# Second attention of a two-block model: probabilities transposed by VectorE in 32x32 squares and carried between partitions by DMAs, in place of TensorE transposes

## The chip, the cores and the metric

The kernel runs on one core of a Trainium2 chip. TensorE (PE, with its weight loads PEld), VectorE (DVE), ScalarE (ACT), GpSimd (POOL) and SyncE (SP, here only a queue that issues DMAs) each work through a list of instructions in order, and wait for one another by semaphores. The metric is the device time of one execution in microseconds (us), taken as the median of several runs.

## The reference

Two blocks of a model on one sequence of 512 tokens with 1024 channels, all in float32. The first block (gated mixing, a long convolution, a stick-breaking attention, a feed-forward layer) is not touched. The second, cut to what matters:

```python
h = rms_norm_2(x, norm_g); proj = h @ w_in            # u, g_rnn, q, k, v, g_attn, m_rnn, m_attn
u = causal_depthwise_conv_2(u, conv_w, conv_b)        # 4 taps
y_rnn = rg_lru(u, ...) * silu(g_rnn)                  # two 128x128 products per block, then a scan
q, k = rope(q), rope(k)                               # 16 query heads, 4 key/value heads
# per block of 128 queries: the 128 keys of the block and the 128 before it, a window of 128
p = exp(scores - m); probs = p / (sum(p) + exp(sink - m))
y_attn = einsum("bnkgqj,bnjkd->bnqkgd", probs, v) * silu(g_attn)
merged = sigmoid(m_rnn) * (y_rnn @ w_rnn_out) + sigmoid(m_attn) * (y_attn @ w_attn_out)
x = rms_norm_2(x + merged @ w_o)
```

## The kernel before

Activations lie as tiles of 128 channels by 512 tokens. Every dense product runs as three float32r matmuls (`mm3`, L293 to L295): the high part of the weight with the high and the low part of the activation, and the low part of the weight with the high part. `project` makes one 128x512 output tile out of eight (or four) weight tiles, so 24 matmuls.

**Weights.** They come as 216 chunks of eight 128x128 tiles (512 KB), in the order of use. `w_load` (L153) issues the DMA of one chunk on the SP queue into one of two `raw` buffers; `w_split` has ACT write the high part `wh` (L169) and DVE the low part `wl` (L170), with three buffers of each. `take` asks for the splits of three chunks and the loads of five. One chunk feeds 24 matmuls.

**Background work.** Attention is written as Python generators (`window_attention`), eight units: two pairs of key/value heads (`kvp`) by four blocks of queries (`n`). A unit makes the scores of two heads (`e`) in two PSUM tiles each (L955, L956), copies them to `S4` (the names `p`), takes maxima, exponentials (L972) and the quotient (L978), transposes the 128x128 probabilities on TensorE (L986, `ident` as the other operand, four per head), copies them out of PSUM (`own`, L987, on ACT; `prev`, L990, on DVE, with a mask, where n > 0), and multiplies with the values (L1000); L1004 puts the result into `ya`. `tick`, called in every `project` after each four weight tiles, advances the generators by a budget (`clk["rate"]`), against the cost that each `yield` names; its second number is a delay in ticks. `finish(*units)` stands ahead of the use of `ya`.

**The order on each engine** is set by a scheduler that works through the instructions by a priority in the order of the program; `urgent()` raises the priority of what stands in it. The stage after the attention starts, L1060 on, has nine rounds: `project` for `u`, a convolution of four taps (L1064 on ACT, three L1066 on DVE), `split` into `uh`, `ul` (L286 and L289), `project` for the gate (`silu2`, L1012, L1013), and `lru` of the round before, whose two products take `uh`, `ul`. Two loops of eight rounds follow, `br` 0 on `yr`, `br` 1 on `ya`, and the last product.

Of the kernel before, what the change touches and what calls it, by code (L numbers as in the profile page):

```python
# [8 lines left out]
F32 = mybir.dt.float32  # L9
F32R = mybir.dt.float32r  # L10
BF16 = mybir.dt.bfloat16
AF = mybir.ActivationFunctionType
ALU = mybir.AluOpType

P = 128
T = 512
# [110 lines left out]
def tile_hybrid_two_block(ctx, tc, xT, wts, prm_d, row_d, sgw_d, rope_d, sink_d, out):  # L127
    nc = tc.nc
    V, A, G, PE = nc.vector, nc.scalar, nc.gpsimd, nc.tensor
# [10 lines left out]
    def bank(tag="mm"):  # L140
        return pm.tile([P, 512], F32, tag=tag, name=nm(tag))
# [101 lines left out]
    ident = const.tile([P, P], F32, name="ident")  # L243
# [10 lines left out]
    class Area:  # L254
# [10 lines left out]
        def tmp(self, dt=F32):  # L265
            return self.tile([P, T], dt)
# [4 lines left out]
    area = [None]  # L271
# [4 lines left out]
    def urgent():  # L276

        return tc.high_priority(offset=URGENT)

    def pr(name, i=0):  # L280
        c = PO[name] + i
        return prm0[:, c : c + 1] if c < n0 else prm[:, c : c + 1]

    def split(src, h, l, eng="a"):
        if eng == "a":
            A.copy(out=h, in_=src)  # L286
        else:
            V.tensor_copy(out=h, in_=src)
        V.tensor_tensor(out=l, in0=src, in1=h.bitcast(F32), op=ALU.subtract)  # L289
# [91 lines left out]
    ps = bank("aux")  # L381
# [114 lines left out]
    for i in range(4):  # L496
        ps = project(hh)
        sg = tmp()
        A.activation(sg, ps, AF.Sigmoid)
        ps = project(hh)  # L500
# [5 lines left out]
    for m in range(4):  # L506
        ps = project(hh)
# [37 lines left out]
    for base in (0, 32):  # L545
# [5 lines left out]
            out=blk, in_=blk, compare_op=ALU.is_ge, fill=0.0, base=0, pattern=[[P, 4], [1, P]],  # L551
# [3 lines left out]
            out=blk, in_=blk, compare_op=ALU.is_ge, fill=0.0, base=63, pattern=[[-P, 4], [-1, P]],  # L555
# [181 lines left out]
    for br, y in enumerate((ya4, acc)):  # L737
# [3 lines left out]
        for m in range(KT):  # L741
            sg = gate(m, br, tmp())
            ps = project(ys)
# [13 lines left out]
    for m in range(KT):  # L757
        ps = project(ys)
# [18 lines left out]
    for m in range(KT):  # L777
        x = tmp()
        nc.sync.dma_start(out=x, in_=xT[m])
        ps = project(mgs)  # L780
# [35 lines left out]
    for m in range(NFF):  # L816
        if m == EARLY:
            finish(norm_task)
        a = up_conv(m, m < EARLY)
        A.activation(a, a, AF.Silu)  # L820
        b = up_conv(m + NFF, m < EARLY)
# [11 lines left out]
    for m in range(KT):  # L833
        ps = project(ffs)
# [6 lines left out]
    VV = area[0].tile([P, NT, 256], F32, "v")  # L841
# [23 lines left out]
    with urgent():  # L865
        ps, pt = mean_sq(S, tok=True, tag="mm")
# [73 lines left out]
    def window_attention(kvp, n):  # L940
        nk = P if n == 0 else 2 * P
        qs = slice(n * P, (n + 1) * P)
        ks = slice((n + 1) * P - nk, (n + 1) * P)
        prs = []
        for e in range(2):
            kv = 2 * kvp + e
            S4 = area[0].tile([P, 4, P], F32, "p")
            prs.append(S4)
            m4, nm4, es, sm = (area[0].tile([P, 4], F32, "s") for _ in range(4))
            per = T // nk  # L950
            for j0 in range(0, 4, per):
                ps = bank("aux")
                for d in range(per):
                    z, q = ps[:, d * nk : (d + 1) * nk], QS[kv][:, j0 + d, qs]
                    PE.matmul(z, lhsT=q, rhs=KS[kvp][:, 2 * e, ks], start=True, stop=False)  # L955
                    PE.matmul(z, lhsT=q, rhs=KS[kvp][:, 2 * e + 1, ks], start=False, stop=True)  # L956
                z = ps.rearrange("p (d k) -> p d k", d=per)
                x = S4[:, j0 : j0 + per]
                if n == 0:
                    V.tensor_tensor(out=x, in0=z, in1=mask[:, 0:1].to_broadcast([P, 4, P]), op=ALU.add)  # L960
                else:
                    A.copy(out=x, in_=z[:, :, P:nk])
                    V.copy_predicated(x, mask[:, 1:2].bitcast(mybir.dt.int32).to_broadcast([P, 2, P]), z[:, :, 0:P])
                yield 0.5, 0
            V.tensor_reduce(out=m4, in_=S4, axis=mybir.AxisListType.X, op=ALU.max)
            sk = sink[:, kv * 4 : kv * 4 + 4]
            V.scalar_tensor_tensor(out=m4, in0=m4, scalar=0.125, in1=sk, op0=ALU.mult, op1=ALU.max)
            V.tensor_scalar(out=nm4, in0=m4, scalar1=-1.0, scalar2=None, op0=ALU.mult)  # L968
            V.tensor_tensor(out=es, in0=sk, in1=m4, op=ALU.subtract)
            A.activation(es, es, AF.Exp)  # L970
            for j in range(4):
                A.activation(  # L972
                    S4[:, j], S4[:, j], AF.Exp, scale=0.125, bias=nm4[:, j : j + 1], accum_out=sm[:, j : j + 1]
                )
            yield 0.95, 1
            V.tensor_tensor(out=sm, in0=sm, in1=es, op=ALU.add)
            V.reciprocal(out=sm, in_=sm)
            V.tensor_tensor(out=S4, in0=S4, in1=sm.unsqueeze(2).to_broadcast([P, 4, P]), op=ALU.mult)  # L978
            yield 0.9, e


        own, prev = [tmp(), tmp()], []
        for e in range(2):
            ps = bank("aux")
            for j in range(4):
                PE.transpose(ps[:, j * P : (j + 1) * P], prs[e][:, j], ident)  # L986
            A.copy(out=own[e], in_=ps)  # L987
            if n > 0:
                prev.append(tmp())
                V.tensor_tensor(  # L990
                    out=prev[e].rearrange("p (a b) -> p a b", a=4), in0=ps.rearrange("p (a b) -> p a b", a=4),
                    in1=mask[:, 2:3].to_broadcast([P, 4, P]), op=ALU.mult,
                )
        yield 1.4 if n else 0.1, 2
        po = bank("aux")
        sums = [(VV[:, n], own)] + ([(VD[:, n - 1], prev)] if n else [])
        for i, (v, w) in enumerate(sums):
            for e in range(2):
                f = kvp * P + e * 64
                PE.matmul(  # L1000
                    po[e * 64 : e * 64 + 64], lhsT=v[:, f : f + 64], rhs=w[e], start=i == 0, stop=i == len(sums) - 1
                )
        y = ya[kvp][:, :, qs]
        V.scalar_tensor_tensor(  # L1004
            out=y, in0=po.rearrange("p (a b) -> p a b", a=4), scalar=0.5, in1=y, op0=ALU.mult, op1=ALU.mult
        )
        yield 0.66, 5
# [52 lines left out]
    for m in range(9):  # L1060
        if m < 8:
            ps = project(h3)
            u = area[0].tile([P, T], F32, "u")
            A.activation(u, ps, AF.Identity, scale=pr("conv_w_2", 24 + m), bias=pr("conv_b_2", m))  # L1064
            for d in (1, 2, 3):
                V.scalar_tensor_tensor(  # L1066
                    out=u[:, d:T], in0=ps[:, 0 : T - d], scalar=pr("conv_w_2", (3 - d) * 8 + m), in1=u[:, d:T],
                    op0=ALU.mult, op1=ALU.add,
                )
            uh, ul = area[0].tile([P, T], F32R, "u"), area[0].tile([P, T], F32R, "u")  # L1070
            split(u, uh, ul)
            silu2(project(h3), yr[m // 4][:, m % 4])
        if late:
            pair.append(lru(*late))
            if len(pair) == 2:
                recurrence(pair)
                pair = []
        late = (m, u, uh, ul)
# [122 lines left out]
```

## Time and profile before

| | us |
|---|---|
| median of 3 runs (1288.71 to 1289.31) | 1288.73 |
| the profiled execution's own time | 1289.3 |
| its span in the profile | 1287.5 |
| PE busy | 1273.9 |
| DVE busy | 869.8 |
| ACT busy | 599.5 |

The span is what the profiler saw from the first instruction to the last; 1.8 us of the execution's own time lie around it. Engines are busy beside one another, so the busy times do not add up. Matmuls are pipelined: each is shown as lasting some 0.39 us, while one starts every 0.23 us, so the cost of a matmul is read from start to start.

### The profile page before, as it was taken

Reading aid. Unit: us, or ns where it says so; the run is one execution under the profiler, and the core shown is the slowest. Engines: PE = TensorE matmul, PEld = TensorE weight load, DVE = VectorE, ACT = ScalarE, POOL = GpSimd, SP = SyncE. Lnnn points to the kernel's source line nnn. Section 1 sums busy time; section 2 is a strip of 40 time slices with the busy share of each in tenths; the row PEclk is TensorE's granted clock in tenths of the full one; section 3 lists DMA queues with packets and bytes.
Section 4 is the critical chain, followed back from the end, with each engine's and each line's share of the span. In section 5 each row is a group of like instructions: output and inputs, shape, how many; then the busy total and the mean of one; then the engine's idle time right before and its main releaser. Section 6 shows DMA issues by size and latency. Waiting matters only on the chain.

```text
span 1287.5 us, 15405 instructions
## 1 busy us (share of the span) xinstructions
PE 1273.9 (99%) x5890; PEld 1034.6 (80%) x5890; DVE 869.8 (68%) x1313; ACT 599.5 (47%) x964; POOL 46.7 (4%) x85
## 2 busy tenths in 40 slices
PE   9999999999999999999999999999999999999997
PEld 7888787778888888888888888888878777788886
DVE  6899998776447597666664333897678895633355
ACT  6733555546324464444443222644568874532232
POOL 0100004320000000000000000000000000000000
PEclk9999999999999999999999999999999999999999
DMA  6332322212333323223333333323223222223341
GB/s 212 131 98 85 96 82 82 66 50 82 98 107 123 131 82 112 91 95 97 97 98 106 115 115 116 99 90 115 83 82 97 67 82 66 81 84 98 131 131 66
DMA packets 39114, 126.80 MB, mean 98 GB/s; under 512 B 4480, under 2 KB 6656, under 8 KB 39040
## 3 DMA queue, kind: packets, MB, share of 16 engines
q1 hardware_dynamic: 37808, 124.76, 30.5%
q8 instruction: 46, 0.75, 0.2%
q10 hardware_dynamic: 1232, 1.05, 0.2%
q14 instruction: 28, 0.23, 0.1%
HBM read 121.60 MB, written 4.19 MB: 98 GB/s over the span
## 4 chain that ended last, share of the span: by engine, by line
PE 96%; DVE 2%; ACT 1%; issue 0%; DMA 0%; POOL 0%; DVEq 0%; SPq 0%; ACTq 0%
PE mm L293 29%; PE mm L294 29%; PE mm L295 29%; PE aux L1000 1%; PE aux L638 1%; PE aux L293 1%; PE aux L295 1%; PE aux L294 1%; PE aux L669 1%; PE aux L955 1%; PE aux L956 1%; PE aux L682 1%; PE aux L986 1%; DVE t L1136 0%; DVE wl L170 0%
## 5 line engine op out<-in xcount | busy, mean ns | idle before, releaser
L293 PE MATMUL mm<-g,wh 128*128 128x512 f32 x1592 | 624.1, 392 | 0.2 <-ACT g L286 0.2
L294 PE MATMUL mm<-g,wh 128*128 128x512 f32 x1592 | 620.6, 390 | 0.0
L295 PE MATMUL mm<-g,wl 128*128 128x512 f32 x1592 | 620.4, 390 | 0.0
L170 DVE TENSOR_TENSOR wl<-raw,wh 128x1024 fp32r<-128x1024 f32 (+1 forms) x212 | 257.8, 1217 | 217.6 <-ACT wh L169 216.9
L169 ACT CAST wh<-raw 128x1024 fp32r<-128x1024 f32 (+1 forms) x211 | 221.4, 1049 | 373.3 <-PE mm L294 276.0
L293 PEld LDWEIGHTS mm<-g,wh 128*128 128x128 f32 x1592 | 299.0, 188 | 67.1 <-issue 4.6
L295 PEld LDWEIGHTS mm<-g,wl 128*128 128x128 f32 x1592 | 299.0, 188 | 63.1 <-issue 0.3
L294 PEld LDWEIGHTS mm<-g,wh 128*128 128x128 f32 x1592 | 299.1, 188 | 60.9 <-DVE g L289 0.4
L490 DVE SCALAR_TENSOR_TENSOR g<-g,prm,g 128x505 f32<-128x505 f32 (+28 forms) x120 | 82.0, 726 | 0.8
L286 ACT CAST g<-t 128x512 fp32r<-128x512 f32 x46 | 28.2, 620 | 64.6 <-DVE t L822 54.3
L809 DVE SCALAR_TENSOR_TENSOR t<-mm,prm,t 128x511 f32<-128x511 f32 x72 | 53.7, 746 | 1.3
L289 DVE TENSOR_TENSOR g<-t,g 128x512 fp32r<-128x512 f32 x46 | 31.7, 696 | 14.3 <-ACT g L286 14.1
L286 ACT CAST g<-g 128x512 fp32r<-128x512 f32 x44 | 25.9, 621 | 24.1 <-DVE g L760 14.2
L972 ACT ACTIVATE p<-p,s 128x128 f32<-128x128 f32 x64 | 24.9, 390 | 21.7 <-DVE s L968 21.7
L820 ACT ACTIVATE t<-t 128x512 f32<-128x512 f32 x22 | 13.9, 633 | 40.4 <-DVE t L809 40.3
L656 DVE TENSOR_TENSOR_SCAN t<-t,zero 128x512 f32<-128x512 f32 (+3 forms) x32 | 27.1, 850 | 7.3 <-POOL t L651 7.2
L289 DVE TENSOR_TENSOR g<-g,g 128x512 fp32r<-128x512 f32 x44 | 28.9, 683 | 2.6 <-ACT g L286 2.1
L807 ACT ACTIVATE t<-mm,prm 128x512 f32<-128x512 f32 x36 | 27.8, 773 | 0.0
L376 ACT ACTIVATE t<-g 128x512 f32<-128x512 f32 (+1 forms) x29 | 17.2, 592 | 20.8 <-DVE g L1115 17.2
L356 ACT ACTIVATE g<-g,prm 128x512 fp32r<-128x512 f32 x24 | 17.2, 718 | 18.0 <-DVE g L768 16.9
L1097 DVE SCALAR_TENSOR_TENSOR t<-t,mm 128x512 f32<-128x512 f32 x8 | 5.5, 688 | 27.1 <-PE mm L295 27.1
L293 PE MATMUL aux<-wh,g 128*128 128x512 f32 (+1 forms) x64 | 21.8, 341 | 0.0
(266 smaller groups left out, 1201.5 us busy)
## 6 DMA issues: line engine op xcount, KB each, us to landing
raw<-in_wts SPq DMA_DIRECT2D x215, 512.0 KB, 3.6
g<-in_xT SPq DMA_DIRECT2D x8, 256.0 KB, 5.8
t<-in_xT SPq DMA_DIRECT2D x8, 256.0 KB, 3.8
spill<-g SPq DMA_DIRECT2D x8, 256.0 KB, 3.3
g<-spill SPq DMA_DIRECT2D x8, 256.0 KB, 4.4
out<-t ACTq DMA_DIRECT2D x4, 256.0 KB, 2.3
out<-t SPq DMA_DIRECT2D x4, 256.0 KB, 2.4
g<-in_row SPq DMA_DIRECT2D x1, 768.0 KB, 6.5
```

The lines of the kernel that those rows point to most:

```text
L169: A.copy(out=h[:, o : o + step], in_=raw[c][:, o : o + step])
L170: V.tensor_tensor(out=l[:, o : o + step], in0=raw[c][:, o : o + step], in1=h[:, o : o + step].bitcast(F32), op=ALU.subtract,)
L286: A.copy(out=h, in_=src)
L289: V.tensor_tensor(out=l, in0=src, in1=h.bitcast(F32), op=ALU.subtract)
L293: PE.matmul(ps, lhsT=lh, rhs=rh, start=start, stop=False)
L294: PE.matmul(ps, lhsT=lh, rhs=rl, start=False, stop=False)
L295: PE.matmul(ps, lhsT=ll, rhs=rh, start=False, stop=stop)
L490: V.scalar_tensor_tensor(out=a[:, d:T], in0=c[:, 0 : T - d], scalar=pr("cv_w", (30 - d) * 4 + i), in1=a[:, d:T], op0=ALU.mult, op1=ALU.add,)
L656: V.tensor_tensor_scan(out=R[:, 0:cx][:, ::-1], data0=F[:, 0:cx][:, ::-1], data1=zero.to_broadcast([P, cx]), initial=1.0, op0=ALU.mult, op ...
L807: A.activation(a, y, AF.Identity, scale=pr("ffn_conv_w", 88 + m), bias=pr("ffn_conv_b", m))
L809: V.scalar_tensor_tensor(out=a[:, d:T], in0=y[:, 0 : T - d], scalar=pr("ffn_conv_w", (2 - d) * 44 + m), in1=a[:, d:T], op0=ALU.mult, op1=A ...
L972: A.activation(S4[:, j], S4[:, j], AF.Exp, scale=0.125, bias=nm4[:, j : j + 1], accum_out=sm[:, j : j + 1])
```

## The change

It transposes each 128x512 tile of probabilities on DVE, in squares of 32x32, into a tile `turned`, and issues 16 DMAs from the SP queue that put the squares into their places in a tile `w`, which is `own`. `prev` is made from `w` instead of from PSUM. In units with n = 0, which have no `prev`, a copy of four columns of `w` onto themselves is left on DVE. The sum takes `prev` first. The costs and delays of the yields are new. The chain that makes `u`, `uh` and `ul` stands in `urgent()`.

```diff
-        prs = []
+        own = []
         for e in range(2):
             kv = 2 * kvp + e
             S4 = area[0].tile([P, 4, P], F32, "p")
-            prs.append(S4)
...
             V.tensor_tensor(out=S4, in0=S4, in1=sm.unsqueeze(2).to_broadcast([P, 4, P]), op=ALU.mult)
-            yield 0.9, e
-
-
-        own, prev = [tmp(), tmp()], []
+            yield 0.7, 0
+
+            turned, w = tmp(), tmp()
+            V.transpose(out=turned, in_=S4.rearrange("p a b -> p (a b)"))
+            own.append(w)
+            src, dst = (x.rearrange("p (a b) -> p a b", a=4) for x in (turned, w))
+            for i in range(4):
+                for j in range(4):
+                    nc.sync.dma_start(
+                        out=dst[32 * j : 32 * j + 32, :, 32 * i : 32 * i + 32],
+                        in_=src[32 * i : 32 * i + 32, :, 32 * j : 32 * j + 32],
+                    )
+            yield 0.7, 5 * e
+
+
+        prev = []
         for e in range(2):
-            ps = bank("aux")
-            for j in range(4):
-                PE.transpose(ps[:, j * P : (j + 1) * P], prs[e][:, j], ident)
-            A.copy(out=own[e], in_=ps)
+            w = own[e].rearrange("p (a b) -> p a b", a=4)
             if n > 0:
                 prev.append(tmp())
                 V.tensor_tensor(
-                    out=prev[e].rearrange("p (a b) -> p a b", a=4), in0=ps.rearrange("p (a b) -> p a b", a=4),
+                    out=prev[e].rearrange("p (a b) -> p a b", a=4), in0=w,
                     in1=mask[:, 2:3].to_broadcast([P, 4, P]), op=ALU.mult,
                 )
-        yield 1.4 if n else 0.1, 2
+            else:
+                w = w[:, 0, 0:P:32]
+                V.tensor_copy(out=w, in_=w)
+        yield 1.4 if n else 0.1, 1
         po = bank("aux")
-        sums = [(VV[:, n], own)] + ([(VD[:, n - 1], prev)] if n else [])
+        sums = ([(VD[:, n - 1], prev)] if n else []) + [(VV[:, n], own)]
...
-            u = area[0].tile([P, T], F32, "u")
...
+            with urgent():
+                u = area[0].tile([P, T], F32, "u")
+                A.activation(u, ps, AF.Identity, scale=pr("conv_w_2", 24 + m), bias=pr("conv_b_2", m))
...
+                uh, ul = area[0].tile([P, T], F32R, "u"), area[0].tile([P, T], F32R, "u")
+                split(u, uh, ul)
             silu2(project(h3), yr[m // 4][:, m % 4])
```

**The chain of the last `u` on DVE (m = 7).** Before, its three steps (L1066) stand apart, a split of weights (L170) and the gate's product (L1013, which waits for the `project` after the one of `u`) between them:

```order
L978 TENSOR_TENSOR p_7997<-p_7997,s_8001 128x512
L1066 SCALAR_TENSOR_TENSOR u_8099<-mm_8059,prm,u_8099 128x511
L170 TENSOR_TENSOR wl_8110<-raw_7983,wh_8109 128x1024
L1066 SCALAR_TENSOR_TENSOR u_8099<-mm_8059,prm,u_8099 128x510
L1013 SCALAR_TENSOR_TENSOR g_7255<-t_8142,mm_8108 128x512
L1066 SCALAR_TENSOR_TENSOR u_8099<-mm_8059,prm,u_8099 128x509
L1038 TENSOR_SCALAR t_8153<-t_8153,s_6344 128x512
L1045 SCALAR_TENSOR_TENSOR t_8154<-t_8154,u_7969 128x512
L289 TENSOR_TENSOR u_8105<-u_8099,u_8104 128x512
```

In the changed kernel the lines are L1078 for the three steps and L998 for `prev`:

```order
L998 TENSOR_TENSOR t_8194<-t_7791,mask_6303 128x512
L1078 SCALAR_TENSOR_TENSOR u_8154<-mm_8104,prm,u_8154 128x511
L1078 SCALAR_TENSOR_TENSOR u_8154<-mm_8104,prm,u_8154 128x510
L1078 SCALAR_TENSOR_TENSOR u_8154<-mm_8104,prm,u_8154 128x509
L1064 TENSOR_TENSOR t_8086<-t_8086,t_8085 128x512
L962 COPY_PREDICATED p_8123<-mask_6303,aux_8147 128x256
L1065 SCALAR_TENSOR_TENSOR t_8090<-t_8090,t_8086 128x512
L170 TENSOR_TENSOR wl_8165<-raw_8028,wh_8164 128x1024
L289 TENSOR_TENSOR u_8160<-u_8154,u_8159 128x512
```

The three steps stand together now, and the gate's product stands behind the whole chain.

**The SP queue at the start of the loop `br` 0.** Before, it holds nothing there but loads of chunks, one for each 24 matmuls. In the changed kernel, where t_8342, t_8425, ... are the tiles `w` of five successive heads (16 DMAs each):

```order
L986 DMA t_8342<-t_8341 32x4x32 x16
L153 DMA raw_8407<-in_wts 128x1024
L986 DMA t_8425<-t_8424 32x4x32 x16
L153 DMA raw_8485<-in_wts 128x1024
L986 DMA t_8503<-t_8502 32x4x32 x16
L986 DMA t_8561<-t_8560 32x4x32 x16
L153 DMA raw_8586<-in_wts 128x1024
L153 DMA raw_8622<-in_wts 128x1024
L986 DMA t_8778<-t_8777 32x4x32 x3
L153 DMA raw_8661<-in_wts 128x1024
```

Chunks raw_8586 and raw_8622 stand behind 48 small DMAs that follow raw_8407.

**The same place on ACT and PE.** ACT before, from the copy-out of one tile's scores (L962) to the next chunk's high part:

```order
L169 CAST wh_8651<-raw_8538 128x1024
L1092 ACTIVATE t_8599<-mm_8600 128x512
L962 COPY p_8675<-aux_8680 128x256
L962 COPY p_8675<-aux_8687 128x256
L972 ACTIVATE p_8675,s_8679<-p_8675,s_8677 128x128
L970 ACTIVATE s_8678<-s_8678 128x4
L972 ACTIVATE p_8675,s_8679<-p_8675,s_8677 128x128 x3
```

ACT in the changed kernel (L961 is the copy-out, L971 the exponentials), ahead of the chunk raw_8586:

```order
L961 COPY p_8796<-aux_8808 128x256
L961 COPY p_8878<-aux_8883 128x256
L961 COPY p_8878<-aux_8890 128x256
L971 ACTIVATE p_8725,s_8729<-p_8725,s_8727 128x128
L969 ACTIVATE s_8728<-s_8728 128x4
L971 ACTIVATE p_8725,s_8729<-p_8725,s_8727 128x128 x3
L969 ACTIVATE s_8799<-s_8799 128x4
L971 ACTIVATE p_8796,s_8800<-p_8796,s_8798 128x128 x3
L169 CAST wh_8657<-raw_8586 128x1024
```

PE in the changed kernel, the end of 32 score matmuls in a row (L954, L955; before, they come in groups of eight with dense matmuls between), one product with the values (L1011), and the next dense tile:

```order
L955 MATMUL aux_8952<-g_6391,g_6501 128x256
L1011 MATMUL aux_8689<-t_8561,v_6184 64x512
L293 MATMUL mm_8755<-g_6380,wh_8657 128x512
L294 MATMUL mm_8755<-g_6382,wh_8657 128x512
L293 MATMUL mm_8859<-g_8251,wh_8695 128x512
L295 MATMUL mm_8755<-g_6380,wl_8658 128x512
```

The scores of four heads stand together ahead of mm_8755, and its weights stand on ACT behind the exponentials of the first two of them.

## Rows read from the trace of the kernel before

**Rows 1.** The page: busy time, share, instructions; then the chain by engine.

```profile
PE 1273.9 (99%) x5890; PEld 1034.6 (80%) x5890; DVE 869.8 (68%) x1313; ACT 599.5 (47%) x964; POOL 46.7 (4%) x85
...
PE 96%; DVE 2%; ACT 1%; issue 0%; DMA 0%; POOL 0%; DVEq 0%; SPq 0%; ACTq 0%
```

**Rows 2.** Timeline of PE at four transposes: start, length (us), line, tile, count.

```profile
1117.82 0.39 PE L295 MATMUL mm<-g,wl 128*128 128x512 f32 x1
1118.05 0.60 PE L986 MATMUL aux<-ident,p 128*128 128x128 f32 x4
1118.40 0.48 PE L293 MATMUL mm<-g,wh 128*128 128x512 f32 x1
1118.72 0.40 PE L294 MATMUL mm<-g,wh 128*128 128x512 f32 x1
```

**Rows 3.** Timeline of PE at the last `u`; in brackets the idle time before.

```profile
1028.33 0.60 PE L986 MATMUL aux<-ident,p 128*128 128x128 f32 x4
1032.11 1.22 PE L293 MATMUL mm<-u,wh 128*128 128x512 f32 x2 [3.18 <-ACT u L286]
...
1035.83 0.39 PE L293 MATMUL mm<-g,wh 128*128 128x512 f32 x1
```

**Rows 4.** SP: issues back to back, one line's issues (ns), its waits.

```profile
1203.30 1.38 SPq L1104 DMA_DIRECT2D g<-spill  x3
...
L153 SPq DMA_DIRECT2D raw<-in_wts x215: 327/328/496, 2.7 to 1244.0; - x108
...
SPq L153 <- DVE wl L170: 1034.3, 200, 15.5
```

**Rows 5.** The chain that ended last, a piece of eight transposes: start, us.

```profile
926.87 0.87 PE aux L986 x8
```

**Rows 6.** Groups by line and shape, 800 to 1135 us: busy us, mean ns, idle before.

```profile
L978 DVE TENSOR_TENSOR p<-p,s 128x512 f32<-128x512 f32 x16 | 11.0, 689 | 0.4
...
L919 DVE STREAM_SHUFFLE t<-mm 128x512 f32<-128x512 f32 x10 | 7.4, 736 | 0.0
...
L169 ACT CAST wh<-raw 128x1024 fp32r<-128x1024 f32 x37 | 38.7, 1046 | 36.5 <-PE mm L294 25.0 <-issue 11.1 <-DMA raw<-in_wts 0.3
L972 ACT ACTIVATE p<-p,s 128x128 f32<-128x128 f32 x64 | 24.9, 390 | 21.7 <-DVE s L968 21.7
```

**Rows 7.** The chain that ended last, 1028 to 1035 us.

```profile
1028.31 1.13 DVE wl L170
1029.44 0.66 DVE u L1066
1030.10 0.59 DVE g L1013
1030.69 0.67 DVE u L1066
...
1034.61 0.43 PE mm L294
```

**Rows 8.** By stretch: PE, PEld, DVE, ACT, POOL busy; then PE's granted clock.

```profile
1030.00:1060.00 30.00, 27.70 (x120) 21.26 (x121) 28.30 (x50) 21.80 (x42) 0.00 (x0) 0.94 0.30 87
```

**Rows 9.** The page: DMA issues, count, KB each, median us to landing.

```profile
raw<-in_wts SPq DMA_DIRECT2D x215, 512.0 KB, 3.6
...
out<-t SPq DMA_DIRECT2D x4, 256.0 KB, 2.4
```

**Rows 10.** Timelines of PE, ACT, DVE: one tile from scores to the quotient.

```profile
1107.82 0.39 PE L955 MATMUL aux<-g,g 128*128 128x256 f32 x1
...
1108.88 0.40 PE L293 MATMUL mm<-g,wh 128*128 128x512 f32 x1
...
1111.53 0.40 ACT L972 ACTIVATE p<-p,s 128x128 f32<-128x128 f32 x1 [2.08 <-DVE s L968]
...
1113.92 0.68 DVE L978 TENSOR_TENSOR p<-p,s 128x512 f32<-128x512 f32 x1
```

**Rows 11.** The page: the queue with the shortest packets; packets, MB, share.

```profile
q10 hardware_dynamic: 1232, 1.05, 0.2%
```

More of the change, by code (lines that the diff above doesn't have):

```diff
@@ L1062, in tile_hybrid_two_block @@
             ps = project(h3)
-            u = area[0].tile([P, T], F32, "u")
[L1064 to L1071, printed above, removed]
+            with urgent():
+                u = area[0].tile([P, T], F32, "u")
+                A.activation(u, ps, AF.Identity, scale=pr("conv_w_2", 24 + m), bias=pr("conv_b_2", m))
+                for d in (1, 2, 3):
+                    V.scalar_tensor_tensor(
+                        out=u[:, d:T], in0=ps[:, 0 : T - d], scalar=pr("conv_w_2", (3 - d) * 8 + m), in1=u[:, d:T],
+                        op0=ALU.mult, op1=ALU.add,
+                    )
+                uh, ul = area[0].tile([P, T], F32R, "u"), area[0].tile([P, T], F32R, "u")
+                split(u, uh, ul)
             silu2(project(h3), yr[m // 4][:, m % 4])
```

## The prediction

> **What bounds the kernel now.** I read the page's busy times and the chain that ended last first: PE is busy for 99% of the span and makes 96% of the chain [rows 1]. So whatever leaves PE shortens the kernel, and whatever makes PE wait lengthens it; work on other engines counts only where PE waits for it. Next I read PE's timeline from 890 to 1130 us, where the eight units run. A dense matmul starts every 0.23 us there. Two things break that pace: groups of four transposes [rows 2], and one stall of 3.18 us at 1028 us, for the last `u` [rows 3]. Last I read SP, since the change puts its DMAs there: SP mostly sits waiting for DVE's split of a chunk (1034 us in 200 waits), and an issue takes 0.33 us [rows 4].
>
> **The change part by part.**
>
> *Transposes leave PE.* A group of four takes 0.35 us to the next dense matmul, which then holds PE for 0.32 instead of 0.23 us: 0.44 [rows 2]; the chain has 0.87 for two groups [rows 5]. There are 16 groups (8 units, 2 heads). The one at 1028.33 lies in the stall and is counted there. Fifteen by 0.44 are 6.6, and at some of them PE waits a little for the quotient, which goes too: I take **6.9 gained**. This is on the path in full. The VectorE page of the Trainium skill ("VectorE: DVE Perf Modes", The three transpose paths and Rules for kernel authors) speaks against the move: it gives 390 ns for a 128x128 transpose on TensorE, and advises TensorE where PSUM will do. With its 390 ns the 64 would be worth 25 us, an estimate; the rows show 0.11 us each, and the sum goes by them.
>
> *ACT loses 16 copies, DVE gains 16 transposes.* Neither bounds the stage as a whole. The nearest DVE rows are a 128x512 product (0.69) and a 128x512 shuffle (0.74) [rows 6], which start some 0.08 less than that apart; I take 0.65. It counts only inside a chain that PE waits for (below), else nothing.
>
> *The `u` chain.* Before, the three steps of the last `u` have a weight split (1.13) and the gate's product (0.59) between them, and PE waits at their end [rows 7]. The stall costs more than its 3.18: behind it matmuls start 0.43 apart [rows 7] instead of 0.23, the level of 1.2 GHz, and the granted clock of that stretch is 0.94 [rows 8]; before the fall PE had idled. Nine matmuls stand between 1032.11 and 1035.83 [rows 3]; at 0.23 behind the transposes (1028.33 + 0.44) they would end at 1030.8, so 5.0 us are lost. In the new order the steps stand together, and PE has a full `project` (24 matmuls, 5.5 us) between its matmuls for `u` and those that use it, against some 4 us of chain. I take **5.0 gained**; the low bound is 3, if DVE, on its way to the last split of `yr`, gives part back.
>
> *The 256 DMAs.* Nothing in the trace has this shape. SP issues others back to back at 1.38 us for three, so 0.475 from start to start; apart, one takes 0.33 [rows 4]. Those are the bounds for a free queue; I take 0.475, as 16 stand in a row. 16 KB should land no later than 256 KB does, in 2.4 [rows 9]. Eight can be in flight (each waits for the eighth before it), which at 2.4 us would allow 0.30 each, so issue decides. A head takes 7.6 us of SP, and is landed 10 us after its transpose. Behind these DMAs stand loads of weights, and on DVE the products for `prev` wait for the landing, with weight splits behind them. A chunk feeds PE for 5.5 us; a load can go about 13 us late before PE misses it (PE is 22 us from a chunk when its load can first go, less 3.6 to land [rows 9], 2.3 to split, and some 3 of waiting for the buffer). Units 0 to 2 stay within that: at most 32 small DMAs (15 us) stand ahead of a load, and it could go 4 us after the first. In `br` 0 five units follow one another within 100 us: 160 DMAs, 76 us of SP, in bursts. Three places come out late:
>
> 1. *Ahead of mm_8755.* Counted from the first of the 32 score matmuls: PE does eight in 1.06 us [rows 10], so is through them at 4.2, and the product with the values at 4.5. Exponentials start 3.7 after a tile's scores [rows 10], 4.1 with other tiles' rows on DVE; seven of 0.39 [rows 6] end at 6.9; the chunk's high part (1.0) is there at 7.9, its low part at 9.6, behind a quotient (0.6), the 32x32 transpose (0.65) and its own 1.13. The chunk itself lands at about 5, so here the order decides, not the landing. PE loses 5.0, and by rows 3 and 7 another 1.8 at the low clock (nine matmuls by 0.2): **6.8 lost** (5.0 if the clock holds).
> 2. *The product of unit 6.* In the same count raw_8760 can go at 16, when the chunk before the last is split; then 56 small DMAs and two loads end at 43.4 and have landed at 45.8; DVE's product ends at 46.4. PE, from 9.2 with 1.8 at the low clock, has 144 dense matmuls (32.8) and 1.3 of products: it asks at 45.1. **1.3 lost** (0 to 5).
> 3. *The end of unit 7,* which now lies five chunks later, right at the first use of `ya`. Counted from its last scores: the first head is transposed at 4.7, 32 DMAs end at 19.9, chunk raw_9346 goes behind them, lands at 23.8 and is split at 26. PE, with 96 dense matmuls (21.8), the products (1.0) and 0.5 of waiting for the second head, asks at 23.3, and finds work for 0.5: **2.8 lost** (1 to 7).
>
> Small waits at units 2 to 4: 0.5. The sum: -6.9 - 5.0 + 6.8 + 1.3 + 2.8 + 0.5 = -0.5, on the profiled execution's own 1289.3: 1288.8. That execution lies 0.6 above the median of the runs, so **1288.3**.
>
> **The rivals.**
>
> *Faster: the weights come in time.* SP issues at 0.40 or less, the clock doesn't fall, and place 1 loses some 3, as the same chain of scores and exponentials ran before without a wait of PE [rows 10]. Then 3.5 are lost in all and 11.9 gained: 1280.3 by the median. For it speaks the issue of 0.33 [rows 4]; against it, three in a row there, and that place 1 hangs on the order.
>
> *Slower: the DMAs come at 0.60 and starve the weights.* One DMA is 32 partitions by four runs of 128 B: 128 runs over 16 engines, eight each, and one packet to report. The shortest packets of the trace take 33 ns (0.2% of 16 x 1287.5 us over 1232, some 850 B each) [rows 11]: nine are 0.30 us a DMA, and hide behind SP. If writes as short as 128 B cost twice that, the engines give 0.60 and decide. Then place 1 is 6 later (48 DMAs by 0.125), place 2 some 2 (the rest hides in time that PE has lost), place 3 four: 12 more, 1300. It decides from a pace of about 0.50 on. The DMA page of the Trainium skill ("DMA: Bandwidth & Descriptors", Specifications) speaks for it: under 512 B an engine reads, modifies and writes. No run here shows this yet.
>
> *DVE becomes the bound in the tail of the `u` stage.* From the `u` of m = 6 to the last split of `yr`, DVE's rows in the order sum to 36 us, 34 before; PE's to 40. If DVE idles 5 us or more among them, for ACT or for a DMA, PE waits at those splits instead of at `u`: 1293.
>
> That the transposes stay on PE can't be: the order has none.
>
> **How the numbers follow.** The forecast has 0.45; with a pace of 0.42 to 0.50 and a clock that falls or not it spans 1284 to 1292. The faster rival has 0.27, the starved weights 0.22, the DVE tail 0.06. Within 0.2% (2.6 us, about what a measurement of this kernel can tell from no change) lies 0.30, all from the forecast; of its rest 0.08 is faster and 0.07 slower. So faster 0.35, same 0.30, slower 0.35. Cases of both signs weigh alike, so the forecast's own range, 1284 to 1292, stands beside the whole: 1281 to 1298 leaves out the faster rival's far half and the worst of the starved weights.
>
> **What would show it.** No L986 on PE, and dense matmuls at 0.23 through its places; no stall for `u` near 1025 us; SP's DMAs starting 0.47 apart and landing in 2 to 3 us; a PE wait of some 5 us ahead of mm_8755, on ACT's `wh` and DVE's `wl`, with a low clock behind it; a shorter one at the first use of `ya`. I am wrong if SP's pace is far from 0.47 either way, if PE waits for `raw` itself, or if DVE sits on a DMA's semaphore in the `u` stage.

## The result, and the profile after

The changed kernel takes 1326.24 us (median of four runs) beside 1289.02 for the kernel before: 1.0287 times as long, with a 95% interval of 1.0273 to 1.0301. It is 37 us slower, 28 us beyond the upper end of the range. The profiled execution spans 1326.7 us against 1287.5.

The page of the changed kernel, busy times and then the chain that ended last by engine and by line (the lines of [rows 1]):

```profile
PE 1283.6 (97%) x5826; PEld 1035.6 (78%) x5826; DVE 877.8 (66%) x1333; ACT 592.2 (45%) x948; POOL 46.7 (4%) x85
...
PE 83%; SPq 9%; DVE 4%; issue 1%; ACT 1%; DMA 1%; POOL 0%; DVEq 0%; ACTq 0%
...
t<-t SPq DMA_DIRECT2D x256, 16.0 KB, 1.8
```

PE has 64 instructions less, the transposes, and is busy for 9.7 us longer: its matmuls ran at a lower clock for part of the time (the mean granted clock is 0.98 against 0.996 before). The new thing is in the chain: SP's queue, 0% before, makes 9% of it. One line of one queue, L986, now sets the end for some 110 us. Its issues, by source line (min/median/max ns, first and last start, and the landing):

```profile
L986 SPq DMA_DIRECT2D t<-t x256: 585/599/1695, 903.2 to 1191.7; - x128
...
DMA to landing us min/median/max: 1.8/1.8/4.8
```

An issue takes 0.585 us at the least and 0.60 in the median, not 0.33, and 16 in a row take 10.24 to 11.12: 0.645 from one to the next. They land 1.8 us after it (4.8 at the most, while eight issues take 5.2), so neither the landing nor the eight in flight hold them. SP's timeline in the last stage (start, length, line, count) shows what that does:

```profile
1064.51 0.53 SPq L153 DMA_DIRECT2D raw<-in_wts  x1
1065.15 10.24 SPq L986 DMA_DIRECT2D t<-t  x16
1075.48 0.53 SPq L153 DMA_DIRECT2D raw<-in_wts  x1
1076.12 21.48 SPq L986 DMA_DIRECT2D t<-t  x32
1097.70 1.01 SPq L153 DMA_DIRECT2D raw<-in_wts  x2
...
1129.39 0.53 SPq L153 DMA_DIRECT2D raw<-in_wts  x1
1130.03 10.24 SPq L986 DMA_DIRECT2D t<-t  x16
1140.37 0.53 SPq L153 DMA_DIRECT2D raw<-in_wts  x1
1141.01 10.24 SPq L986 DMA_DIRECT2D t<-t  x16
```

In these lines SP is solid with issues, and between two loads of weights stand 16 or 32 small DMAs. There a load goes some 11 us or more after the one before it, while PE uses a chunk up in 5.5 (only from 1097 to 1113 us, left out above, do loads follow faster). That reads on as a wait on ACT (from 890 to 1210 us; 0.3 us in the kernel before), and as three kinds of wait on PE (engine, line, what it waited for: us, times, longest):

```profile
ACT wh L169 <- DMA raw<-in_wts: 84.2, 17, 15.1
```

```profile
PE aux L1011 <- DVE t L998: 14.8, 4, 8.0
PE mm L293 <- ACT wh L169: 11.9, 4, 5.7
PE aux L1011 <- DVE t L1004: 3.6, 1, 3.6
PE mm L293 <- ACT t L1104: 1.8, 1, 1.8
```

L169 splits a chunk that landed late; L998 and L1004 wait on DVE for squares that landed late; L1104 stands on ACT behind a split that waits for its chunk. All come from SP. The first in time, right behind the first unit's product, on PE's timeline:

```profile
935.43 1.08 PE L1011 MATMUL aux<-t,v 128*64 128x512 f32 x4
942.20 0.79 PE L293 MATMUL mm<-g,wh 128*128 128x512 f32 x1 [5.69 <-ACT wh L169]
942.79 0.63 PE L294 MATMUL mm<-g,wh 128*128 128x512 f32 x1
```

After the gap matmuls start 0.43 apart, the 1.2 GHz level, as behind the stall of [rows 3]. In the worst stretch the granted clock (the 0.83; columns as in [rows 8]) is well below the 0.94 there, with PE busy for 19 of 30 us:

```profile
1130.00:1160.00 30.00, 19.22 (x64) 11.21 (x63) 8.48 (x10) 5.16 (x6) 0.00 (x0) 0.83 0.35 88
```

To see where the time goes by stage I use one instruction that every kernel has: ACT's first step of the last `u` (the `A.activation` into `u`; L1064 before, L1076 after). Its line in the changed kernel, and in the best kernel found below (e8):

```profile
L1076 ACT ACTIVATE u<-mm,prm x8: 762/774/781, 925.3 to 1023.3; 128x512 f32<-128x512 f32 x8
```

```profile
L1078 ACT ACTIVATE u<-mm,prm x8: 764/768/782, 926.1 to 1015.9; 128x512 f32<-128x512 f32 x8
```

The last start, and from there to the end of the span, in us:

| kernel | last `u` at | from there to the end |
|---|---|---|
| before | 1026.4 | 261.1 |
| changed | 1023.3 | 303.4 |
| e3, 12 DMAs a head | 1016.2 | 277.6 |
| e10, 14 DMAs a head | 1018.7 | 289.6 |
| e4, GpSimd copies | 1014.6 | 278.5 |
| e7, GpSimd issues | 1015.1 | 283.9 |
| e8, through DRAM | 1015.9 | 262.6 |
| e11, e8 with SP loaded | 1022.3 | 292.8 |

Against e8 the changed kernel loses 7.4 us up to the last `u` (the gap at 942) and 40.8 behind it, in the first pass of the last stage and at its end, where five units follow one another. PE runs the same 5826 instructions in both:

```profile
PE 1268.0 (99%) x5826; PEld 1027.9 (80%) x5826; DVE 878.2 (69%) x1333; ACT 590.6 (46%) x948; POOL 46.0 (4%) x85
```

So of the 48.2 us between the two spans 32.6 are idle time of PE (43.1 in the changed kernel, 10.5 in e8), and 15.6 a longer busy time for the same work: behind the gaps its matmuls start 0.43 apart, as above, in place of 0.23.

### The profile page after: what moved, and what is told of

It reads as the page before. It is cut to its first block, busy times and chain, and to the rows that moved or that the text cites. A ratio compares the mean times of both kernels' runs of the same rounds, so it can differ in the third digit from the quotient of the medians.

```text
span 1326.7 us, 15692 instructions
## 1 busy us (share of the span) xinstructions
PE 1283.6 (97%) x5826; PEld 1035.6 (78%) x5826; DVE 877.8 (66%) x1333; ACT 592.2 (45%) x948; POOL 46.7 (4%) x85
## 4 chain that ended last, share of the span: by engine, by line
PE 83%; SPq 9%; DVE 4%; issue 1%; ACT 1%; DMA 1%; POOL 0%; DVEq 0%; ACTq 0%
PE mm L293 26%; PE mm L294 25%; PE mm L295 25%; SPq L986 8%; PE aux L1011 1%; DMA raw<-in_wts 1%; PE aux L638 1%; PE aux L293 1%; PE aux L295 1%; PE aux L294 1%; DVE wl L170 1%; PE aux L669 1%; PE aux L682 1%; DMA t<-t 0%; DVE t L1148 0%
## 5 line engine op out<-in xcount | busy, mean ns | idle before, releaser
L293 PE MATMUL mm<-g,wh 128*128 128x512 f32 x1592 | 628.6, 395 | 14.2 <-ACT wh L169 11.9
L169 ACT CAST wh<-raw 128x1024 fp32r<-128x1024 f32 (+1 forms) x211 | 221.5, 1050 | 415.3 <-PE mm L294 235.7
L170 DVE TENSOR_TENSOR wl<-raw,wh 128x1024 fp32r<-128x1024 f32 (+1 forms) x212 | 257.8, 1217 | 224.0 <-ACT wh L169 223.4
L971 ACT ACTIVATE p<-p,s 128x128 f32<-128x128 f32 x64 | 24.9, 390 | 6.2 <-DVE s L967 5.9
L1011 PE MATMUL aux<-t,vd 128*64 128x512 f32 x24 | 11.4, 694 | 14.8 <-DVE t L998 14.8
L998 DVE TENSOR_TENSOR t<-t,mask 128x512 f32<-128x512 f32 x12 | 8.1, 686 | 24.6 <-DMA t<-t 24.6
```

The lines of the kernel that those rows point to most:

```text
L169: A.copy(out=h[:, o : o + step], in_=raw[c][:, o : o + step])
L170: V.tensor_tensor(out=l[:, o : o + step], in0=raw[c][:, o : o + step], in1=h[:, o : o + step].bitcast(F32), op=ALU.subtract,)
L293: PE.matmul(ps, lhsT=lh, rhs=rh, start=start, stop=False)
```

## The experiments

Theory A was that SP's pace alone broke the sum; theory B, that the sum also missed waits that do not hang on SP. The kernel before was run again beside each group: 1288.60 (e1 to e4), 1289.01 (e5 to e8), 1288.89 (e9 to e12).

**e1 and e2: the `u` chain alone, and undone.** e1 is the kernel before with the second part of the diff only:

```diff
+            with urgent():
                 u = area[0].tile([P, T], F32, "u")
...
                 split(u, uh, ul)
```

> The kernel before, with one part of the change alone: the u chain of each m stands together and ahead (priority), transposes stay on TensorE, no small DMAs. My term of the prediction: the stall of 3.18 us at 1028 us and its low clock go, 5.0 gained, 1284.0. Rival: the stall only moves to the next product that VectorE is late for, and the time stays within 1 us of 1289.

Measured: 1285.72, ratio 0.9976 (0.9967 to 0.9985), 2.9 us faster. Its span is 3.7 shorter, and no wait for `u` is left on PE. The mechanism holds; the size of 5.0 was too large. Some 0.7 of it came back at once, as a longer wait of PE at another transpose (0.93 in place of 0.24).

e2 takes that `with` out of the changed kernel.

> The changed kernel without its second part: the u chain stands where it stood before. If the 5.0 are gained in the changed kernel too, it goes to about 1331. If TensorE's waits for weights hide that chain, it stays within 1.5 us of 1326. If putting the u chain ahead is itself part of the loss (weight splits pushed behind it), it comes out faster than 1324.

Measured: 1326.61, no different from 1326.24. In the changed kernel that part gives nothing. The old stall of 3.18 us at this place is 0.8 even without it:

```profile
PE mm L293 <- ACT u L286: 0.8, 1, 0.8
```

**e3: 12 DMAs for a head.** The pace of the trace, on fewer DMAs, gives the SP time that my sum had.

```diff
             for i in range(4):
+                d = slice(32 * i, 32 * i + 32)
+                G.tensor_copy(out=dst[d, :, d], in_=src[d, :, d])
                 for j in range(4):
-                    nc.sync.dma_start(
+                    if j != i:
+                        nc.sync.dma_start(
...
```

> 12 DMAs for each head in place of 16: the four squares that stay on their own partitions are copied by the idle GpSimd. With 0.645 us for an issue, as the changed kernel's trace has it, a head then holds SP for 7.7 us, which is just the 7.6 us (16 by 0.475) of my sum. Theory A, that SP's pace is the whole fault of the sum: 1284 to 1292, as forecast. Theory B, that the sum also missed waits that do not hang on the pace (VectorE held at the products behind the landing, the place of the units in the order): above 1300. In between, both.

Measured: 1294.76, 6.2 above the kernel before (0.5%, 0.34 to 0.64). A quarter of the DMAs less gives back 31 us of 37. So the pace is most of the error, but not all: with the SP time that I had assumed the sum is still 6.7 short. PE waits for products, 9.9 us in seven places, and never for a chunk. One thing moves with the count: the order is planned with the DMAs in it, and the 32 score matmuls in a row of the changed kernel are broken up here, as in e4, e6, e7, e8 and e9; e5 and e11 have the 32 in a row, e10 20 and e12 28 (by their traces 16 and 4, 25 and 3, with two dense matmuls between).

**e4: no small DMAs; GpSimd copies the squares.**

```diff
-                    nc.sync.dma_start(
+                    G.tensor_copy(
```

> No small DMAs at all: the 16 squares of a head are moved by 16 copies on the idle GpSimd, which can write other partitions than it reads; SP has only the weights again. Theory A (weights come late because SP issues the small DMAs): no wait of TensorE for a weight chunk is left, and the time is 1278 to 1286, the 11.9 gained less some 2 to 4 for the chain ahead of mm_8755. Theory B (the loss lies in the order and in VectorE's wait for the moved squares): above 1300, with the products' waits still there.

Measured: 1297.32. No wait of PE for a chunk is left, as A says, yet the time lies between the ranges of A and B, 2.6 us above e3. GpSimd needs 0.405 us for a copy on average, 13 us for the two heads of a unit, and PE asks for the product earlier:

```profile
PE aux L1011 <- DVE t L998: 11.7, 3, 6.9
```

So part of B is real: a unit's squares must be through by the time its product stands in the order, whoever moves them. Beside e8 below, where PE waits for no squares, this kernel loses 18.0 us.

**e5: the same DMAs with runs of 512 bytes.** Order and count stay; only the runs change (`prev` and the product read the new order of columns; those lines are left out).

```diff
-            V.transpose(out=turned, in_=S4.rearrange("p a b -> p (a b)"))
+            V.transpose(
+                out=turned.rearrange("p (j a c) -> p a j c", j=4, a=4), in_=S4.rearrange("p a (j c) -> p a j c", j=4)
+            )
...
-                        out=dst[32 * j : 32 * j + 32, :, 32 * i : 32 * i + 32],
-                        in_=src[32 * i : 32 * i + 32, :, 32 * j : 32 * j + 32],
+                        out=w[32 * j : 32 * j + 32, P * i : P * i + P],
+                        in_=turned[32 * i : 32 * i + 32, P * j : P * j + P],
```

> The changed kernel with the same 16 DMAs of 16 KB for each head, in the same order on SP and TensorE, but each moves 32 rows of 512 bytes in place of 128 runs of 128 bytes (the transposed squares are written, and read by the product, in another order of columns). It tells what sets the 0.60 us of an issue, and what the pace alone does to the time with the order kept. If SP's time for an issue comes from the number of runs: 0.33 to 0.45 us, no wait for a weight chunk, and 1280 to 1294. If it belongs to any DMA between partitions: 0.60 again and 1324 to 1328.

Measured: 1324.59. The issue, by source line:

```profile
L987 SPq DMA_DIRECT2D t<-t x256: 507/588/1781, 903.0 to 1185.5; - x128
```

A quarter of the runs, and 0.588 instead of 0.599 us; the time is in the range given for any DMA between partitions. The price is not one of short runs, nor, by the same number, of the work that each run is for the DMA engines.

**e6: the product later.** e4, with one number changed.

```diff
-            yield 0.7, 5 * e
+            yield 0.7, 9 * e
```

> The kernel with the squares moved by GpSimd (no small DMAs, 1297.3), with one number changed: the step that multiplies the moved squares comes 9 ticks after the second head's transpose in place of 5 (a tick is 12 matmuls, 2.73 us). Theory B1: what is left there (11.7 us of idle TensorE in 3 places, and the low clock behind two of them) is the product asked for before 32 moves are through; with 24 us in place of 13 those waits go, and the time is 1280 to 1287. Rival: the units' end is pushed onto the first use of ya, where TensorE waits instead: 1292 to 1300.

Measured: 1298.17. The rival was right. The waits only move, to the products of the last two units, at 1140 and at 1157 to 1163 us: 9.5 us in three places, where e4 has 11.7.

**e7: GpSimd issues the DMAs.**

```diff
-                    nc.sync.dma_start(
+                    nc.gpsimd.dma_start(
```

> The changed kernel with its 256 small DMAs issued by the idle GpSimd in place of SP, so that no weight load stands behind one. If 0.6 us is the price of this DMA on any queue, it comes out as with GpSimd's copies, 1292 to 1302: no waits for weights, those for the products stay. If GpSimd takes 1 us or more for an issue, the products come later still: above 1305. If the weights' late arrival came from the DMA engines (128-byte writes in their way) and not from SP, the waits for weights stay and the time is above 1315.

Measured: 1301.07, within the first theory's 1292 to 1302. An issue on GpSimd takes 0.551 us (median of 256), PE waits for no chunk, and 11.3 us of waits for squares stay. The same DMAs on another queue cost 25 us less, so that part of the loss goes with SP's queue and not with the traffic (the order changes too, as said at e3). The rest, 12 us above the kernel before and 21.8 above e8, stays without SP; it is in the main squares that come late.

**e8: through DRAM, 5 DMAs a head.** From e5:

```diff
-            for i in range(4):
-                for j in range(4):
-                    nc.sync.dma_start(
-                        out=w[32 * j : 32 * j + 32, P * i : P * i + P],
-                        in_=turned[32 * i : 32 * i + 32, P * j : P * j + P],
-                    )
+            there = dp.tile([P, T], F32, name=nm("there"))
+            nc.sync.dma_start(out=there, in_=turned)
+            for j in range(4):
+                nc.sync.dma_start(
+                    out=w[32 * j : 32 * j + 32].rearrange("r (i x) -> r i x", i=4),
+                    in_=there[:, P * j : P * j + P].rearrange("(i r) x -> r i x", i=4),
+                )
```

> The changed kernel with 5 DMAs for each head in place of 16: one writes the transposed squares to DRAM (256 KB), four read them back to their partitions (64 KB each, runs of 512 bytes). SP waits for the write to land (2.4 us) before the reads go, so a head holds SP for some 4 to 5 us, against 10.3 with 16 small DMAs. By theory A weights are in time and it lies near the kernel with 12 DMAs or below: 1284 to 1296. If SP's waiting for the write delays weights as much as the issues do: above 1300.

Measured: 1279.31, ratio 0.9925 (0.9910 to 0.9939), below the range that I gave and 9.7 us faster than the kernel before. One head on SP, the write, a load of weights in between, the four reads:

```profile
1100.34 0.34 SPq L986 DMA_DIRECT2D there<-t  x1
1102.46 0.35 SPq L153 DMA_DIRECT2D raw<-in_wts  x1
1102.86 2.21 SPq L988 DMA_DIRECT2D t<-there  x4
```

SP issues for 2.0 to 3.1 us a head in place of 10.3, and here a load fills the wait for the write. The largest waits of PE that are left:

```profile
PE aux L383 <- DVE zero L237: 1.3, 1, 1.3
PE mm L294 <- DVE g L289: 0.5, 1, 0.5
```

**e9: e8 without the `u` part,** the same `with` taken out.

> The kernel that sends the squares through DRAM (1279.3), without the u chain's part: what the transposes' leaving TensorE is worth by itself. By my term of 6.9: 1281.7 to 1282.7, and 2.5 to 3.5 slower than with the u chain, as that part gave 2.9 alone. If most of its 9.5 us came from the u chain: 1285 or more.

Measured: 1279.52, ratio 0.9928. Both guesses on the split were wrong: the `u` part is worth nothing here, and the first part gives all of the 9.4 us. The stall for `u` is gone without it: PE waits nowhere for `u` in e9. Why was not tested; the units stand elsewhere in the order. PE's line of the page:

```profile
PE 1267.1 (99%) x5826; PEld 1027.6 (80%) x5826; DVE 878.4 (69%) x1333; ACT 590.6 (46%) x948; POOL 46.7 (4%) x85
```

Its span is 9.9 us shorter than before: 6.8 of PE's busy time (the transposes, and the low clock behind the old stall) and 3.1 of its idle time (the stall was 3.18). These shares are read from the two pages, not measured apart.

**e10: 14 DMAs a head** (as e3, with copies for `i < 2` only).

> 14 DMAs for each head in place of 16 (two squares by GpSimd), on SP. Theory A2: ten of the 16 heads fall into the first eight chunks pairs of the last stage (87 us of TensorE), and there SP itself is the bound: 160 issues by 0.645 are 103 us, with the weights' 24 loads some 115. Two fewer for each head take 12.9 off there and half of the 7.3 lost earlier: 1306 to 1312. Rival: it is the order (32 score matmuls in a row) that costs, and with it broken up (20 in a row here) the time is that of 12 DMAs, 1293 to 1298.

Measured: 1310.29, inside the 1306 to 1312 of theory A2. By the table above, the last part takes 15.0, 27.0 and 40.8 us more than e8's with 12, 14 and 16 DMAs a head: 6.0 and 6.9 for each DMA more. Ten heads fall there, and ten issues are 6.45 us. So beyond 12 each issue more is paid about in full, as it would be where SP is the bound; what the order adds (20 and 32 score matmuls) is in these differences too, and they leave little for it. SP does not bound the whole stretch: in the chain that ended last its small DMAs make 54% from 1050 to 1200 us in the changed kernel, and 35% from 1045 to 1190 in e10.

**e11: squares early, SP loaded.** e8 with eleven DMAs more behind the five of each head:

```diff
+            more = S4.rearrange("p a b -> p (a b)")
+            for i in range(11):
+                a, b = divmod(i, 4)
+                nc.sync.dma_start(
+                    out=more[32 * b : 32 * b + 32, P * a : P * a + P],
+                    in_=turned[32 * a : 32 * a + 32, P * b : P * b + P],
+                )
```

> The kernel through DRAM (1279.3), with 11 more DMAs of 16 KB between partitions issued on SP behind each head's five; what they write is read by nobody. The squares are early as there, SP's work for a head is again that of the changed kernel (2.1 and 11 by 0.645 are 9.2 us, and the wait for the write), and the order has the 32 score matmuls in a row again. Theory A2 (SP's hours are the bound): 1305 to 1325, with TensorE waiting for weight chunks. Rival (the loss is products waiting for their own squares): at most the 6.8 that I had put on the order at the first place, 1279 to 1288.

Measured: 1316.76, 37.5 above e8, although a unit's own squares come before the added DMAs. PE's waits are now the chunks' kind:

```profile
PE mm L293 <- ACT t L1113: 12.2, 1, 12.2
PE mm L293 <- ACT wh L169: 11.0, 3, 4.9
PE aux L1020 <- DVE t L1013: 2.1, 1, 2.1
```

The 12.2 is the same cause one step on; ACT's timeline just before it:

```profile
1129.90 1.05 ACT L169 CAST wh<-raw 128x1024 fp32r<-128x1024 f32 x1 [14.34 <-DMA raw<-in_wts]
1141.13 1.04 ACT L169 CAST wh<-raw 128x1024 fp32r<-128x1024 f32 x1 [10.18 <-DMA raw<-in_wts]
1142.08 1.08 ACT L1113 ACTIVATE t<-mm 128x512 f32<-128x512 f32 x2
```

ACT sits on two late chunks for 24 us; the tanh that empties a PSUM bank stands behind them, and PE waits for the bank.

**e12: what the 0.60 belongs to.** e8 with six DMAs of other shapes a head (`more` is the head's finished `S4`, as in e11, and `flat` a tile in DRAM):

```diff
+            nc.sync.dma_start(out=more[:, 0 : 2 * P], in_=turned[:, 0 : 2 * P])
+            nc.sync.dma_start(out=more[0:32, 2 * P : 3 * P], in_=turned[0:32, 0:P])
+            nc.sync.dma_start(out=more[64:96, 2 * P : 3 * P], in_=turned[0:32, 0:P])
+            nc.sync.dma_start(out=more[:, 3 * P : 4 * P], in_=turned[:, 0:P])
+            nc.sync.dma_start(out=flat[0:32, 0:P], in_=turned[0:32, 0:P])
+            nc.sync.dma_start(out=more[96:128, 2 * P : 3 * P], in_=there[0:32, 0:P])
```

> The kernel through DRAM with six more DMAs for each head, read by nobody, each of another shape: 128 partitions to 128 within SBUF (128 KB and 64 KB), 32 to the same 32, 32 to other 32 partitions, 32 partitions to DRAM, DRAM to 32 partitions (16 KB each). Their issue times tell what the 0.60 us belongs to. Theory: to both ends in SBUF, so the first four take 0.6 and the last two 0.33. Rivals: to 32 partitions as the source (then the first and fourth take 0.33, the fifth 0.6); to crossing partitions (then only the fourth of them, 32 to other 32, takes 0.6). The order has 28 score matmuls in a row with SP lightly loaded (5 us a head): if that order costs 6.8 as I had it, 1285 to 1288, else 1279 to 1283.

Measured: 1287.75. The six by source line, in the order of the diff:

```profile
L994 SPq DMA_DIRECT2D p<-t x16: 512/514/1010, 903.5 to 1145.9; - x16
...
L995 SPq DMA_DIRECT2D p<-t x16: 561/573/613, 904.1 to 1146.5; - x16
...
L996 SPq DMA_DIRECT2D p<-t x16: 575/586/1429, 904.8 to 1147.1; - x16
...
L997 SPq DMA_DIRECT2D p<-t x16: 542/570/598, 905.4 to 1147.8; - x16
...
L998 SPq DMA_DIRECT2D flat<-t x16: 427/428/587, 908.9 to 1150.4; - x16
...
L999 SPq DMA_DIRECT2D p<-there x16: 419/419/422, 909.3 to 1150.9; - x16
```

With both ends in SBUF an issue takes 0.51 to 0.59 us: 128 KB on 128 partitions as well as 16 KB on 32, crossing partitions or not. With one end in DRAM it takes 0.42 here (the theory had 0.33, which is what a 256 KB write and a weight load take when they stand apart). The order's own cost stays open: this kernel has 28 score matmuls nearly in a row and is 8.4 above e8, but it also has six issues a head more, and its one large wait (4.5 us) is again ACT behind a late chunk. Behind the 28 PE waits for 0.18 us only; but there ACT makes the chunk's high part ahead of the exponentials, not behind them as at the prediction's place 1. So the 28 cost 8.4 here at the most, and the order of place 1 was not run without late chunks.

## Why the prediction was wrong

*What held.* The transposes and their copies are off PE and ACT, no chain for `u` stalls PE, landing is short and issue decides. The gains were of about the right size: 11.9 in the sum, 9.4 measured (e9). But the split was not: what I gave to the `u` chain (5.0) is worth 2.9 alone and nothing beside the first part (e1, e2, e9). By e9's busy and idle time the first part's 9.4 is near its own 6.9 and the stall, which goes with it. The 390 ns that the prediction quotes from the Trainium skill's "VectorE: DVE Perf Modes" (The three transpose paths) is that page's figure for bf16, and these transposes are float32; the sum did not use it.

*The step that failed* is the price of an issue: 0.475 from start to start, with 0.33 and 0.475 as the bounds for a free queue and 0.60 left to a rival, where the trace has 0.645. Both bounds were rows of the wrong kind: every DMA in the kernel before has an end in DRAM. For one with both ends in SBUF the trace of before had nothing near, so those rows bounded nothing from above, and the range should have said so. Why such an issue takes longer stays open; e5 and e12 show only what it does not go by: the runs, the bytes, crossing partitions.

*The second failure, and the larger in us,* is how a slow pace was priced. My slow rival had 0.60, near the truth, and gave 1300: 12 us, from three places. It stood beside a count that decides the matter without any place: 160 DMAs in the first pass of the last stage, whose 16 chunks of 5.5 us take PE 88 us. At 0.475 they are 76 us of SP, and fit with 16 loads beside them; at 0.60 they are 96, at 0.645 103, and SP has more to do than PE. With the loads (0.53 each there) it is 112, an excess of 24 us, and from there on each DMA more costs about its whole issue time (e10). The rest of the 40.8 is near the 15.0 that e3 loses in the same part, where the same sum is 86, just under PE's; with 14 DMAs a head it gives 11 and 15 for the 27.0 of e10. That sum was made after the runs. "It decides from a pace of about 0.50 on" agrees with the count (no run has a pace between 0.475 and 0.645); what follows beyond it was not a shift of three waits.

*The rival's cause was wrong, too.* It put the pace on the DMA engines and short writes. The Trainium skill's "DMA: Bandwidth & Descriptors" (Specifications) has read-modify-write below 512 bytes; e5 moves 512-byte runs at nearly the same pace (0.588 us an issue), so that rule does not set the time here. The Trainium skill's page "Perfetto Trace Analysis" (What "DMA-bound" means) names the case that the trace does show, an issuing queue that is solid with DMA slices, and says that large descriptors are what matters; e5's, four times as long, took the issue from 0.599 to 0.588 only, and rows of 1024 bytes in e12 still take 0.514. Fewer DMAs, each with an end in DRAM, were the remedy (e8).

*Units 0 to 2* were to stay within 13 us of slack "at most 32 small DMAs (15 us) stand ahead of a load". Up to 937.33 there are 32 in a row, 21.69 us, and PE waits 5.69: the rule held, the pace broke it. With 12 a head that wait is not there, with 14 it is 1.3 (e10).

*The three places.* Place 1 lies behind the 32 score matmuls (1090.87 to 1095.32). The waits there, and the one ahead of them, on PE's timeline:

```profile
1080.52 0.79 PE L293 MATMUL mm<-g,wh 128*128 128x512 f32 x1 [3.85 <-ACT wh L169]
...
1099.16 1.97 PE L1011 MATMUL aux<-t,v 128*64 128x512 f32 x2 [3.57 <-DVE t L1004]
1102.62 0.80 PE L293 MATMUL mm<-g,wh 128*128 128x512 f32 x1 [1.48 <-ACT wh L169]
...
1104.71 0.80 PE L293 MATMUL mm<-g,wh 128*128 128x512 f32 x1 [0.87 <-ACT wh L169]
```

The 5.9 us at place 1 are near the 5.0 that I had, but that is luck: 3.57 are for squares that landed late, where I had the product with the values wait for nothing, and ahead of the split of mm_8755's chunk ACT waits for its landing (0.88 us), where I had said that the order decides and not the landing. The 3.85 at 1080.52, for a late chunk, stand in no place of the prediction. Whether the order by itself costs the 6.8 is open (e12). Places 2 and 3, the products of the last units, wait for squares as described (8.0, and 1.9 and 4.0 us), larger by the pace. (Place 3's own figures, 26 less 23.3 and less 0.5 of work, give 2.2 and not 2.8.) Even with my SP time (e3) the waits and what hangs on them are 15 us behind the last `u`, where I had 11.

## What to carry to other kernels

Before adding many small DMAs to a queue, sum the queue's hours per stage (count by issue time, plus the loads it already issues) and set them against the bound engine's time in that stage; if the sum can pass it within the uncertainty of the price, reckon beyond that point with the whole excess, not with a few waits, and with what the moved data's own lateness costs beside it (15 us here, e3). A price from rows of another kind (DRAM to SBUF for SBUF to SBUF) is no bound. And cut the number of DMAs rather than their bytes: here one write to DRAM and four reads in place of 16 moves turned a loss of 37 us into a gain of 9.7.

## What the runs showed of the hardware

- An issue of a DMA between two places in SBUF took 0.51 to 0.60 us on SP (medians of five shapes, 16 to 128 KB) and 0.55 on GpSimd's queue (16 KB); with one end in DRAM 0.33 alone, 0.42 to 0.43 behind another, and 0.53 for a load of weights right behind a row of the small ones.
- A round through DRAM was quicker than 16 direct moves: the write landed in 2.4 us and the reads in 3.1 (medians of e8), against 10.3 us for the issues alone.
- GpSimd copied a 32x128 square to other partitions in 0.29 us (median; 0.405 on average), so the squares can move without any DMA, though not fast enough here.
